# Root-mean-square sums one dq projection later, their diagonals on GpSimd, one 512-column broadcast matmul for each factor

## The chip, the core and the metric

The kernel runs on one core of a Trainium2 chip. The metric is the time of one execution in microseconds (us) on the device; lower is better. TensorE (PE) does matmuls and transposes, VectorE (DVE) and ScalarE (ACT) work on tiles in SBUF and PSUM, GpSimd (POOL) on tiles in SBUF, and SyncE (SP) issues most of the DMAs. Each engine runs its own queue in order, so an instruction that waits holds up all that stands behind it on that engine.

## What is computed

Two transformer layers (`DEPTH = 2`) over 512 tokens of width 1024. Each layer has a mixer of two attention groups (MLA with a low-rank q and kv; DSA with an index score and a top-k choice of keys) and a mixture of 16 experts. What matters here is the beginning of the mixer:

```python
def rms_norm(x, g):
    y = xf * lax.rsqrt(jnp.mean(jnp.square(xf), axis=-1, keepdims=True) + RMS_EPS)
    return (y * g.astype(jnp.float32)).astype(x.dtype)
...
    q = (rms_norm(qa, q_norm_g) @ w_q_up).reshape(B, T, MLA_HEADS, MLA_NOPE + MLA_ROPE)
    c_kv = rms_norm(kva, kv_norm_g)
...
        score = jnp.where(key_idx[None, None, :] <= tq[None, :, None], score, -jnp.inf)
        _, sel = lax.top_k(score, n_keep)
...
    proj = h @ w_in
    qa, kva, kr, dq, dk, dv, iq, ik, iw = jnp.split(proj, SPLIT_POINTS, axis=-1)
```

Here qa has 384 columns, kva 256, dq 512, and `n_keep` is 128.

## The kernel before, in words

All activations are held transposed, features on the partitions and the 512 tokens along the columns. The projection `h @ w_in` is cut into 13 column tiles of 128 features: `proj(ct)` makes one in PSUM with 24 matmuls of 512 columns (`project`, L271: eight slices of the width, each in three products of a high and a low part). The tiles come in the order S, two of iq, DKV, two of kva, three of qa, four of dq. PSUM tiles of the name `mm` rotate through four banks, `pv` through two. SBUF tiles made by `u4` share nine slots, and a tile waits until the last reader of the slot's earlier tile is done.

After qa the squares of kva (`sqk`, the two added up by GpSimd) and of qa (`sqq`, and a part of the tile `dkv`) are summed over the features: matmuls of one column each against ones (L418) put 8 sums for each token of a block on the partitions. In the program this stands in the loop over the four dq tiles at `i == 0`. L421 and L422 (DVE) turn the sums into means plus epsilon, `rsqrt` (L185, GpSimd) takes the power -0.5 of 128 x 8 numbers.

At `i == 2` the factors, which lie along the partitions, are spread over all partitions along the columns: for each of 2 factors and 4 blocks of 128 tokens DVE makes a diagonal matrix (L431, identity times factor), and TensorE multiplies a matrix of ones with it (L432). `bc[0]`, the kv factor, scales `kvg` (L437), which ACT and GpSimd then split into `ckv`. `bc[1]`, the q factor times -96^-0.5, goes into the tile `ct` (L441, L442), by which every q of the MLA heads is multiplied (L528).

Beside all this DVE does the top-k of the DSA group. For query blocks 1, 2 and 3 (tiles of 256, 384 and 512 columns) it runs 16 pairs of MAX8 (L365, the eight largest) and MATCH_REPLACE (L366, strike them out) in strict sequence, and then makes the distance mask `dd` (L372). These pairs have a lowered priority (`LOWER`), so the scheduler fills DVE's queue with them between other work. Each dq tile is read out of PSUM twice: by ACT (L405, the high part) and then by DVE (L406, the low part, which needs ACT's result), and both parts are copied by DMA into the layout of the heads.

The order on every engine is written at build time: a scheduler lists the instructions by priority and by its own estimate of times. Nothing is chosen at run time.

Of the kernel before, what the change touches and what calls it, by code (L numbers as in the profile page):

```python
# [13 lines left out]
AF = mybir.ActivationFunctionType  # L14
OP = mybir.AluOpType
# [3 lines left out]
NT = T // 128  # L19
# [13 lines left out]
SC_MLA = 96.0 ** -0.5  # L33
# [62 lines left out]
def block_kernel(ctx, tc, xT0, x0, win, wqk, wuv, wo, gvec, lnp, rw, rb, wgu, wdn, consts, angles, stripd, rowsd, out):  # L96
    nc = tc.nc
# [19 lines left out]
    def C(name, a=0, b=None):  # L117
        o, w = _C[name]
        return cn[:, o + a:o + (w if b is None else b)]

    ident = C("id")
# [11 lines left out]
    def u4(name, dt=F32):  # L133
        return sl.tile([128, 1024], dt, name=name, tag="u4", bufs=NU4)
# [4 lines left out]
    def u4p(name, dt=F32):  # L139
        t = u4(name, dt)  # L140
        return t[:, :512], t[:, 512:]
# [11 lines left out]
    def ps(tag):  # L153
        return psp.tile([128, 512], F32, name=tag, bufs={"mm": 4, "tr": 2, "pv": 2}[tag])
# [12 lines left out]
    def copy_rows(out, src):  # L167
        nc.sync.dma_start(out.bitcast(F32), src.bitcast(F32))
# [13 lines left out]
    def rsqrt(v, n, tag):  # L182

        y = sm.tile([128, n], F32, name=tag + "y")
        return y, nc.gpsimd.tensor_tensor(y, v, mhalf[:, :n], op=OP.pow).ins  # L185

    def transpose4(src, c0, tag="tr"):
        p = ps(tag)
        for k in range(4):
            last_T[0] = nc.tensor.transpose(p[:, k * 128:(k + 1) * 128], src[:, c0 + k * 128:c0 + (k + 1) * 128],  # L190
                                            ident).ins
        return p
# [38 lines left out]
    def attention(l, xh, xl, wraw, first, rest, x_dram):  # L231
# [10 lines left out]
        def proj(ct):  # L242
            if l and ct == 0:

                raw((3 + AHEAD) // 2)
                for c in range(4):
                    done[c] = ps("mm" if c > 1 else "tr")
                for a in range(2):
                    if a:
                        rest()  # L250
                    for c in (0, 2):
                        order = (0, 1, 2) if a else (0, 2, 1)
                        for j in order:
                            for d in (c, c + 1):
                                project(done[d], first[d], slice(256 * a, 256 * (a + 1)), (j,), order[2])
            if ct not in done:
                done[ct] = ps("mm")
                project(done[ct], weights(ct), slice(0, T))
            return done.pop(ct)
# [16 lines left out]
        acs, acm, adist = at[:, :512], at[:, 512:768].bitcast(BF), at[:, 768:].bitcast(F16)  # L276
# [9 lines left out]
        p = proj(T_S)  # L286
# [9 lines left out]
        for i in range(2):  # L296
            p = proj(T_IQ + i)
# [8 lines left out]
        p = proj(T_DKV)  # L306
# [7 lines left out]
        p = ps("mm")  # L314
# [6 lines left out]
        p = transpose4(dkv, 0)  # L321
        nc.scalar.copy(dvt, p.rearrange("p (a b) -> p a b", a=NT)[:, :, 64:128])
        p = transpose4(S, 0)
# [15 lines left out]
        for i in range(1, NT):  # L339
            n = 128 * (i + 1)  # L340
            acc, work = u4p("aw")
            rel = None
            for h in range(8):
                if (i, h) in KVA_AT:
                    latents(KVA_AT.index((i, h)))
                p = ps("mm")
                nc.tensor.matmul(p[:, :n], iq[h // 4][:, h % 4, (i - 1) * 128:i * 128], ik4[:, :n],
                                 start=True, stop=True)
# [5 lines left out]
                if h == 0:  # L354
                    nc.vector.scalar_tensor_tensor(acc[:, :n], r[:, :n], w, acm[:, 384 - 128 * i:],
                                                   op0=OP.mult, op1=OP.subtract)
                else:
                    nc.vector.scalar_tensor_tensor(acc[:, :n], r[:, :n], w, acc[:, :n],  # L358
                                                   op0=OP.mult, op1=OP.add)
# [10 lines left out]
            for dd in DD[i]:  # L370
# [3 lines left out]
                                               op0=OP.mult, op1=OP.add)  # L374
# [9 lines left out]
        for i in range(3):  # L384
            p = proj(T_QA + i)
# [16 lines left out]
        for i in range(4):  # L402
            p = proj(T_DQ + i)
            qh, ql = u4p("dq", F32R)
            nc.scalar.activation(qh, p, AF.Copy, scale=-0.125)  # L405
            nc.vector.scalar_tensor_tensor(ql, p, -0.125, qh.bitcast(F32), op0=OP.mult, op1=OP.subtract)  # L406
            for s in range(2):
                d = dqs[i // 2][:, i % 2 * 2 + s, :]
                for j, q in enumerate((qh, ql)):
                    b = 64 * (s ^ j)  # L410
                    copy_rows(d[b:b + 64], q[64 * s:64 * (s + 1)])
            if i == 0:

                p = ps("pv")
                for j, qq in enumerate((sqk[:1], sqq)):
                    for t in range(NT):
                        for q in qq:
                            nc.tensor.matmul(p[:, j * 4 + t:j * 4 + t + 1], q[:, t * 128:(t + 1) * 128],  # L418
                                             C("ones", 0, 1), start=(q is qq[0]), stop=(q is qq[-1]))
                ms = sm.tile([128, 8], F32, name="ms")  # L420
                nc.vector.tensor_scalar(ms[:, 0:4], p[:, 0:4], 1.0 / 256, 1e-6, op0=OP.mult, op1=OP.add)  # L421
                nc.vector.tensor_scalar(ms[:, 4:8], p[:, 4:8], 1.0 / 384, 1e-6, op0=OP.mult, op1=OP.add)  # L422
                rs, _ = rsqrt(ms, 8, "rms")
            if i == 2:
                bc = []
                dgt = u4("dg")
                for j, f in ((0, 1.0), (1, -SC_MLA)):
                    p = ps("pv")
                    for t in range(NT):
                        dg = dgt[:, j * 512 + t * 128:j * 512 + (t + 1) * 128]  # L430
                        nc.vector.tensor_scalar(dg, ident, rs[:, j * 4 + t:j * 4 + t + 1], f, op0=OP.mult, op1=OP.mult)  # L431
                        nc.tensor.matmul(p[:, t * 128:(t + 1) * 128], C("ones"), dg, start=True, stop=True)  # L432
                    bc.append(p)
        ckt = bigt(F32R)
        ckv = [(ckt[:, 1024 * i:1024 * i + 512], ckt[:, 1024 * i + 512:1024 * (i + 1)]) for i in range(2)]
# [2 lines left out]
            split(*ckv[i], kvg[i], nc.gpsimd)  # L438
        cte, cto = u4p("ct")
        for c, a, b in ((cte, 0, 64), (cto, 64, 0)):  # L440
            nc.scalar.copy(c[a:a + 64], bc[1][a:a + 64])  # L441
            nc.vector.tensor_mul(c[b:b + 64], acs[b:b + 64], bc[1][b:b + 64])  # L442

        zz = u4("zz")
        with tc.issue_after(anchor):
# [4 lines left out]
        for t in range(NT):  # L450
            p = ps("mm")
# [150 lines left out]
        g, b = ln  # L602
# [5 lines left out]
        p = ps("pv")  # L608
# [127 lines left out]
        for s in range(16):  # L736
            if s >= LAG:
                t, k = 2 * ((s - LAG) // 8) + 1, (s - LAG) % 8
# [11 lines left out]
            t, k = 2 * (s // 8), s % 8  # L750
# [661 lines left out]
    for a, b in [(0, 512), (512, 1024), (1024, 2048), (2048, 3072), (3072, 4096)]:  # L1412
        d = a // 2048, (slice(None), slice(a % 2048, a % 2048 + b - a))
        nc.sync.dma_start(xf[d[0]][d[1]], xT0[:, a:b])
        if a >= w_at:
            c = w_at // 2048, (slice(None), slice(w_at % 2048, w_at % 2048 + 1024))
# [7 lines left out]
    for l in range(L):  # L1424
        r, pre = attention(l, xh, xl, wraw, ws, rest, src)
        y = experts(l, r, pre)
        wraw = pre["win"]
        new = combine(l, r, *y, pre["x1"], wraw)
        if l + 1 < L:
            xh, xl, rest, ws = new  # L1430
        src = x1d
# [59 lines left out]
```

## Time and profile before

| what | us |
| --- | --- |
| median of 3 runs | 1238.58 |
| lowest, highest | 1237.5, 1240.96 |
| profiled execution, its own time | 1238.69 |
| its span in the trace | 1236.9 |

Over the span PE is busy 1168.2 us (94%), DVE 1033.9 (84%), ACT 803.8 (65%), POOL 292.6 (24%). Layer 0 begins at 0 and layer 1 at about 620 us; in each, the stretch that the change touches is some 35 us long (77 to 110 us, 693 to 726 us). A busy PE is not PE at its peak: the ends of matmuls are modelled and they overlap, so the matmuls' start times tell more. The clock that the throttle granted to TensorE is given as a share of full speed.

### The profile page before, as it was taken

The numbers are of one execution on the slowest core, as the hardware profiler recorded it, in microseconds if no ns is written. First come the engines' busy times: TensorE is split into PE (matmuls) and PEld (weight loads), VectorE is DVE, ScalarE is ACT, GpSimd is POOL, SyncE is SP. The second block draws the span as 40 slices with busy tenths as digits, with TensorE's granted clock in tenths as the row PEclk, the third lists the DMA queues.
The fourth block names the chain that finished last, engine by engine and source line by source line (L and its number), as shares of the span: only waits on it lengthen the run. The fifth ranks groups of instructions, "written<-read, shape, count | busy, mean of one in ns | idle before, by whom it ended". The sixth has DMA issues, their size and how long they took to land.

```text
span 1236.9 us, 16946 instructions
## 1 busy us (share of the span) xinstructions
PE 1168.2 (94%) x5777; PEld 918.9 (74%) x5777; DVE 1033.9 (84%) x1875; ACT 803.8 (65%) x1264; POOL 292.6 (24%) x233
## 2 busy tenths in 40 slices
PE   8999999998999999999898998999989999999995
PEld 6677565787788888887686775557877888888873
DVE  4699958398999999988857999673889999999887
ACT  4523668444888888887534245684448888888873
POOL 2334123210211111200543342321201111121005
PEclk9989989999999999999988899999999999999998
DMA  7615204366999999997336161044669999999841
GB/s 269 187 60 172 85 1 137 136 238 236 371 384 392 384 378 377 376 327 272 95 124 167 41 203 43 3 144 164 236 247 368 389 382 390 392 373 362 307 170 68
DMA packets 56972, 292.21 MB, mean 236 GB/s; under 512 B 10063, under 2 KB 13903, under 8 KB 28464
## 3 DMA queue, kind: packets, MB, share of 16 engines
q1 hardware_dynamic: 47376, 270.48, 59.4%
q0 software_dynamic: 8064, 15.36, 3.4%
q10 hardware_dynamic: 1440, 5.24, 1.0%
q8 instruction: 47, 0.77, 0.2%
q14 instruction: 45, 0.37, 0.1%
HBM read 267.96 MB, written 31.98 MB: 242 GB/s over the span
## 4 chain that ended last, share of the span: by engine, by line
PE 56%; DVE 10%; issue 4%; POOL 2%; DMA 2%; ACT 2%; POOLq 0%; DVEq 0%; ACTq 0%
PE pv L1081 14%; PE mm L1059 13%; PE mm L1060 13%; PE tr L190 4%; PE mm L631 3%; PE mm L271 2%; PE pv L509 2%; PE tr L500 2%; DVE aw L366 1%; DMA xg<-xdr,ii 1%; POOL x L1214 1%; DVE m L365 1%; PE mm L543 1%; DVE aw L358 1%; PE pv L655 1%
## 5 line engine op out<-in xcount | busy, mean ns | idle before, releaser
L163 ACT CAST hl<-big 128x1024 fp32r<-128x1024 f32 x438 | 457.6, 1054 | 132.5 <-PE mm L1060 62.7
L164 DVE TENSOR_TENSOR hl<-big,hl 128x1024 fp32r<-128x1024 f32 x403 | 485.8, 1229 | 57.0 <-ACT hl L163 49.4
L1059 PE MATMUL mm<-hl,xh 128*128 128x512 f32 x504 | 207.1, 411 | 0.0
L1060 PE MATMUL mm<-hl,xh 128*128 128x512 f32 x504 | 197.3, 391 | 0.0
L1081 PE MATMUL pv<-hl,hT 128*128 128x512 f32 x720 | 173.0, 395 | 4.1 <-DVE big L1091 4.1
L1081 PEld LDWEIGHTS pv<-hl,hT 128*128 128x128 f32 x720 | 137.2, 191 | 33.9 <-DVE big L1091 4.8
L271 PE MATMUL mm<-big,hl 128*128 128x512 f32 (+1 forms) x624 | 145.2, 392 | 3.1 <-ACT hl L163 1.9
L271 PEld LDWEIGHTS mm<-big,hl 128*128 128x128 f32 x624 | 116.1, 199 | 28.3 <-ACT hl L163 3.9
L164 POOL TENSOR_TENSOR hl<-big,hl 128x1024 fp32r<-128x1024 f32 x35 | 85.4, 2443 | 162.7 <-ACT hl L163 154.4
L1023 POOL DMA_INDIRECT xg<-xdr,ii x30 | 52.4, 1746 | 282.7 <-DVE ii L1037 253.9
L1060 PEld LDWEIGHTS mm<-hl,xh 128*128 128x128 f32 x504 | 95.2, 189 | 15.8
L1059 PEld LDWEIGHTS mm<-hl,xh 128*128 128x128 f32 x504 | 95.0, 188 | 15.5
L1060 PE MATMUL mm<-hl,xl 128*128 128x512 f32 x252 | 98.7, 392 | 0.0
L1059 PE MATMUL mm<-hl,xl 128*128 128x512 f32 x252 | 98.5, 391 | 0.0
L631 PE MATMUL mm<-hl,big 128*128 128x512 f32 x384 | 94.5, 397 | 0.0
L490 ACT ACTIVATE P<-P,mn 128x128 f32<-128x128 f32 (+3 forms) x128 | 71.7, 566 | 13.2 <-DVE mn L488 10.8
L631 PEld LDWEIGHTS mm<-hl,big 128*128 128x128 f32 x384 | 70.3, 188 | 13.2
L502 ACT COPY big<-tr 128x512 f32<-128x512 f32 (+3 forms) x128 | 50.1, 431 | 32.2 <-PE tr L500 31.2
L500 PEld LDWEIGHTS tr<-cn,P 128*128 128x128 f32 x320 | 36.4, 141 | 38.8 <-ACT big L502 21.2
L500 PE MATMUL tr<-cn,P 128*128 128x128 f32 x320 | 59.7, 292 | 4.8 <-DVE P L496 3.2
L570 POOL TENSOR_TENSOR mh<-dd,cn 128x256 f32<-128x256 f32 (+2 forms) x64 | 43.5, 701 | 77.1 <-DVE q L528 21.1
L1101 POOL DMA_INDIRECT ydr<-y,ii x26 | 26.5, 1018 | 146.7 <-ACT y L1097 123.1
(278 smaller groups left out, 1884.7 us busy)
## 6 DMA issues: line engine op xcount, KB each, us to landing
big<-wgu SPq DMA_DIRECT2D x128, 1024.0 KB, 7.7
big<-wdn SPq DMA_DIRECT2D x64, 1024.0 KB, 7.3
big<-win SPq DMA_DIRECT2D x10, 1024.0 KB, 5.8
ydr<-zz SPq DMA_DIRECT2D x2, 4096.0 KB, 13.4
big<-wo SPq DMA_DIRECT2D x8, 1024.0 KB, 9.9
big<-ydr SPq DMA_DIRECT2D x8, 1024.0 KB, 4.9
big<-wqk SPq DMA_DIRECT2D x4, 1024.0 KB, 5.0
big<-dq SPq DMA_DIRECT2D x32, 128.0 KB, 2.3
```

The costliest lines, as they stand in the source:

```text
L163: i = nc.scalar.copy(hi, src).ins
L164: (eng or nc.vector).tensor_sub(lo, src, hi.bitcast(F32))
L190: last_T[0] = nc.tensor.transpose(p[:, k * 128:(k + 1) * 128], src[:, c0 + k * 128:c0 + (k + 1) * 128], ident).ins
L271: nc.tensor.matmul(p[:, ts], w[j == 1][:, k * 128:(k + 1) * 128], x, start=(j + k == 0), stop=(j == end and k == 7))
L490: nc.scalar.activation(e, e, AF.Exp, bias=mn[:, i:i + 1], scale=-1.0, accum_out=su[:, i:i + 1])
L500: nc.tensor.transpose(p[:, (i - kb) * 128:(i - kb + 1) * 128], P[:, PO[i] + kb * 128:PO[i] + (kb + 1) * 128], ident)
L502: copies.append(nc.scalar.copy(pt[kb], p[:, :512 - 128 * kb]).ins)
L631: R["pe"] = nc.tensor.matmul(pp[t][i], x, w[:, i * 512:(i + 1) * 512], start=first, stop=last).ins
L1023: return nc.gpsimd.indirect_dma_start(out=st[e]["xg"], out_offset=None, in_=xdr[l], in_offset=bass.IndirectOffsetOnAxis(ap=st[e]["ii"][:, ...
L1059: nc.tensor.matmul(pg, x, w[:, :512], start=(k == 0 and x is a and w is wh), stop=last)
L1060: nc.tensor.matmul(pu, x, w[:, 512:], start=(k == 0 and x is a and w is wh), stop=last)
L1081: nc.tensor.matmul(py[i], x, w[:, i * 512:(i + 1) * 512], start=(k == 0 and x is a and w is wh), stop=last)
```

## The change

The sums (L418), the means and the power move from the first turn of the dq loop to the second. The diagonals move there too, from DVE to GpSimd: two products of 128 x 512, each with the identity repeated four times as one operand and the factors repeated along the columns as the other. At `i == 2` one matmul of 512 columns for each factor takes the place of four of 128. The constant -96^-0.5 leaves the diagonals and goes into the two instructions that make `ct` (on ACT a scale, on DVE a fused scalar).

```diff
-            if i == 0:
+            if i == 1:
                 p = ps("pv")
 ...
-                nc.vector.tensor_scalar(ms[:, 0:4], p[:, 0:4], 1.0 / 256, 1e-6, op0=OP.mult, op1=OP.add)
-                nc.vector.tensor_scalar(ms[:, 4:8], p[:, 4:8], 1.0 / 384, 1e-6, op0=OP.mult, op1=OP.add)
+                for j, n in enumerate((256, 384)):
+                    nc.vector.tensor_scalar(ms[:, 4 * j:4 * j + 4], p[:, 4 * j:4 * j + 4], 1.0 / n, 1e-6,
+                                            op0=OP.mult, op1=OP.add)
                 rs, _ = rsqrt(ms, 8, "rms")
+                dgt = u4("dg")
+                for j in range(2):
+                    nc.gpsimd.tensor_tensor(dgt[:, j * 512:(j + 1) * 512].rearrange("p (t a) -> p t a", t=NT),
+                                            ident[:, None, :].to_broadcast([128, NT, 128]),
+                                            rs[:, 4 * j:4 * j + 4][:, :, None].to_broadcast([128, NT, 128]), op=OP.mult)
             if i == 2:
                 bc = []
-                dgt = u4("dg")
-                for j, f in ((0, 1.0), (1, -SC_MLA)):
+                for j in range(2):
                     p = ps("pv")
-                    for t in range(NT):
-                        dg = dgt[:, j * 512 + t * 128:j * 512 + (t + 1) * 128]
-                        nc.vector.tensor_scalar(dg, ident, rs[:, j * 4 + t:j * 4 + t + 1], f, op0=OP.mult, op1=OP.mult)
-                        nc.tensor.matmul(p[:, t * 128:(t + 1) * 128], C("ones"), dg, start=True, stop=True)
+                    nc.tensor.matmul(p, C("ones"), dgt[:, j * 512:(j + 1) * 512], start=True, stop=True)
                     bc.append(p)
 ...
-            nc.scalar.copy(c[a:a + 64], bc[1][a:a + 64])
-            nc.vector.tensor_mul(c[b:b + 64], acs[b:b + 64], bc[1][b:b + 64])
+            nc.scalar.activation(c[a:a + 64], bc[1][a:a + 64], AF.Copy, scale=-SC_MLA)
+            nc.vector.scalar_tensor_tensor(c[b:b + 64], bc[1][b:b + 64], -SC_MLA, acs[b:b + 64], op0=OP.mult, op1=OP.mult)
```

The new lines are L422 (means), L427 (diagonals), L434 (broadcast), L439 (`kvg`), L443 and L444 (`ct`); behind these, lines of the changed kernel stand two higher than before (L528 is L530).

How the order moves is seen at three places; both layers read alike there.

First, TensorE around the sums. The rows marked with - are those of before. L271 are the projections (24 a tile: 96 are three qa tiles and the first dq), L418 the sums, of which four (of `sqk`) stand further up in both.

```order
 L347 MATMUL mm<-ik,big 128x512 x3
-L271 MATMUL mm<-big,hl 128x512 x96
+L271 MATMUL mm<-big,hl 128x512 x120
 L418 MATMUL pv<-cn,sqq 128x1 x2
 L418 MATMUL pv<-cn,dkv 128x1
```

The second dq projection now stands ahead of the sums. Behind them, still on TensorE:

```order
 L418 MATMUL pv<-cn,sqq 128x1 x2
 L418 MATMUL pv<-cn,dkv 128x1
-L271 MATMUL mm<-big,hl 128x512 x52
-L432 MATMUL pv<-dg,cn 128x128 x2
-L271 MATMUL mm<-big,hl 128x512 x2
-L432 MATMUL pv<-dg,cn 128x128 x6
-L271 MATMUL mm<-big,hl 128x512 x18
+L271 MATMUL mm<-big,hl 128x512 x24
+L434 MATMUL pv<-dg,cn 128x512 x2
+L271 MATMUL mm<-big,hl 128x512 x24
```

The broadcasts stood inside the fourth dq projection, and now stand between the third and the fourth.

Second, DVE at the means, in query block 2's top-k (the number in a name such as m_493 counts the pairs up). Before:

```order
L365 MAX m_493<-aw 128x8
L421 TENSOR_SCALAR ms<-pv 128x4
L422 TENSOR_SCALAR ms<-pv 128x4
L366 MATCH_REPLACE aw<-m_493,aw 128x384
L365 MAX m_496<-aw 128x8
L406 SCALAR_TENSOR_TENSOR dq<-mm,dq 128x512
```

With the change:

```order
L365 MAX m_493<-aw 128x8
L366 MATCH_REPLACE aw<-m_493,aw 128x384
L365 MAX m_496<-aw 128x8
L366 MATCH_REPLACE aw<-m_496,aw 128x384
L365 MAX m_499<-aw 128x8
L406 SCALAR_TENSOR_TENSOR dq<-mm,dq 128x512
L366 MATCH_REPLACE aw<-m_499,aw 128x384
L365 MAX m_502<-aw 128x8
L366 MATCH_REPLACE aw<-m_502,aw 128x384
L365 MAX m_505<-aw 128x8
L422 TENSOR_SCALAR ms<-pv 128x4 x2
```

The means have moved behind four more pairs and behind the low part of the first dq tile. On GpSimd the split of the weights `wv` (L164), which stood behind the power, now stands ahead of it, and the first L405 on ACT waits for that split, whose slot its tile takes, where it waited for the last sum before.

Third, DVE at the diagonals. Before:

```order
L366 MATCH_REPLACE aw<-m_517,aw 128x384
L431 TENSOR_SCALAR dg<-cn,rmsy 128x128 x2
L406 SCALAR_TENSOR_TENSOR dq<-mm,dq 128x512
L431 TENSOR_SCALAR dg<-cn,rmsy 128x128 x6
L437 TENSOR_TENSOR kvg<-kvg,pv 128x512 x2
L365 MAX m_520<-aw 128x8
```

With the change:

```order
L366 MATCH_REPLACE aw<-m_517,aw 128x384
L365 MAX m_520<-aw 128x8
L406 SCALAR_TENSOR_TENSOR dq<-mm,dq 128x512
L439 TENSOR_TENSOR kvg<-kvg,pv 128x512 x2
L366 MATCH_REPLACE aw<-m_520,aw 128x384
```

The eight diagonals have left DVE's queue. Further down the fourth L406 stands two instructions later than before (a mask L372 and a replace of 512 columns have come ahead of it), one more pair of 512 columns stands ahead of the first q (L528, now L530), and in the middle heads PE, DVE, ACT and POOL have another order: the mask of query block 3 comes ahead of a q product and a weight split that stood ahead of it before. From the last heads on, the order is the same again.

## Rows read from the trace of the kernel before

**Rows 1.** Stretches: us, busy PE PEld DVE ACT POOL, PEclk, DMA share, GB/s.

```profile
77.40:110.50 33.10, 28.59 (x116) 23.84 (x117) 28.31 (x70) 9.17 (x15) 14.58 (x8) 0.79 0.21 48
110.50:160.00 49.50, 45.74 (x193) 31.26 (x193) 45.34 (x128) 28.34 (x74) 17.30 (x20) 0.94 0.38 139
305.00:620.00 315.00, 306.84 (x1517) 251.32 (x1516) 292.85 (x357) 254.84 (x300) 60.18 (x40) 0.99 0.89 337
```

**Rows 2.** Chain that ended last, layer 1: start us, us, what.

```profile
715.13 2.35 DVE dg L431
```

**Rows 3.** Timeline of DVE, layer 0: start, us, instruction [idle before <-releaser].

```profile
84.98 0.16 DVE L421 TENSOR_SCALAR ms<-pv 128x4 f32<-128x4 f32 x1 [0.28 <-PE pv L418]
...
87.48 0.56 DVE L365 MAX8 m<-aw 128x8 f32<-128x384 f32 x1
...
88.73 0.56 DVE L365 MAX8 m<-aw 128x8 f32<-128x384 f32 x1
...
93.52 0.69 DVE L406 SCALAR_TENSOR_TENSOR dq<-mm,dq 128x512 fp32r<-128x512 f32 x1 [2.31 <-ACT dq L405]
...
99.00 0.48 DVE L431 TENSOR_SCALAR dg<-cn,rmsy 128x128 f32<-128x128 f32 x2
...
99.99 3.41 DVE L431 TENSOR_SCALAR dg<-cn,rmsy 128x128 f32<-128x128 f32 x6
...
110.51 0.69 DVE L406 SCALAR_TENSOR_TENSOR dq<-mm,dq 128x512 fp32r<-128x512 f32 x1 [1.35 <-ACT dq L405]
...
113.82 0.68 DVE L365 MAX8 m<-aw 128x8 f32<-128x512 f32 x1
...
115.32 0.69 DVE L365 MAX8 m<-aw 128x8 f32<-128x512 f32 x1
...
118.23 0.68 DVE L528 TENSOR_TENSOR q<-mm,ct 128x512 f32<-128x512 f32 x1
```

**Rows 4.** Timeline of DVE, layer 1, the same places.

```profile
708.57 0.69 DVE L406 SCALAR_TENSOR_TENSOR dq<-mm,dq 128x512 fp32r<-128x512 f32 x1 [1.63 <-ACT dq L405]
...
714.05 0.48 DVE L431 TENSOR_SCALAR dg<-cn,rmsy 128x128 f32<-128x128 f32 x2
...
715.04 3.40 DVE L431 TENSOR_SCALAR dg<-cn,rmsy 128x128 f32<-128x128 f32 x6
...
725.56 0.69 DVE L406 SCALAR_TENSOR_TENSOR dq<-mm,dq 128x512 fp32r<-128x512 f32 x1 [1.08 <-ACT dq L405]
...
733.28 0.68 DVE L528 TENSOR_TENSOR q<-mm,ct 128x512 f32<-128x512 f32 x1
```

**Rows 5.** Timeline of PE, layer 0.

```profile
54.90 21.95 PE L271 MATMUL mm<-big,hl 128*128 128x512 f32 x96
77.49 0.38 PE L418 MATMUL pv<-cn,sqq 128*128 128x1 f32 x2 [0.64 <-ACT sqq L389]
...
80.52 0.59 PE L418 MATMUL pv<-cn,dkv 128*128 128x1 f32 x2 [1.99 <-ACT dkv L389]
...
84.80 14.33 PE L271 MATMUL mm<-big,hl 128*128 128x512 f32 x52
...
195.24 1.02 PE L543 MATMUL mm<-ke,q 128*128 128x512 f32 x2
```

**Rows 6.** Costliest lines, shapes apart, POOL: busy us, mean ns of one, idle before.

```profile
L570 POOL TENSOR_TENSOR mh<-dd,cn 128x384 f32<-128x384 f32 x32 | 27.8, 887 | 77.1 <-DVE q L528 21.1 <-DVE rc L492 18.8 <-DVE mn L488 18.7
...
L164 POOL TENSOR_TENSOR big<-kvg,big 128x512 fp32r<-128x512 f32 x4 | 5.1, 1287 | 5.0 <-ACT big L163 5.0
...
L185 POOL TENSOR_TENSOR rmsy<-ms,mhalf 128x8 f32<-128x8 f32 x2 | 3.3, 1654 | 6.1 <-DVE ms L422 6.1
```

**Rows 7.** Timeline of POOL, layer 0.

```profile
79.68 2.36 POOL L164 TENSOR_TENSOR hl<-big,hl 128x1024 fp32r<-128x1024 f32 x1 [9.39 <-ACT hl L163]
...
99.99 2.35 POOL L164 TENSOR_TENSOR hl<-big,hl 128x1024 fp32r<-128x1024 f32 x1 [3.10 <-ACT hl L163]
```

**Rows 8.** Timeline of DVE, layer 0, behind the last mask of the top-k.

```profile
156.59 0.69 DVE L488 CUSTOM_DVE_ANT_0 P<-mm,mh 128x512 f32<-128x512 f32 x1 [1.22 <-POOL mh L570]
```

## Prediction

> **What bounds the kernel now.** I read the busy times by stretch first. In the stretch from the first means to the fourth dq tile of layer 0 no engine is full: TensorE is busy 28.6 of 33.1 us at a granted clock of 0.79, so that it ran partly at the lower of its two levels, and VectorE 28.3 us [rows 1]. From there to 160 us VectorE is busy 45.3 of 49.5 us, 92%, with top-k pairs between the work of the heads [rows 1]. In the experts (305 to 620 us) TensorE is busy 306.8 of 315 us at 0.99 [rows 1]. So VectorE's queue sets the pace of attention until the top-k is done, and what is gained there reaches the end of the run: behind it stands TensorE's own work, which starts that much earlier, with DMA at 0.89 of its time and not full. The chain of waits says the same from the other end: it runs through VectorE's diagonals for 2.35 us in layer 1 [rows 2].
>
> The timeline of VectorE then shows where its queue stood still. In layer 0 it waits 0.28 us for the sums, 2.31 for the second dq tile and 1.35 for the fourth [rows 3]; in layer 1, 1.63 and 1.08 [rows 4]. On TensorE the reader sees why: the sums come while ACT is still squaring, so TensorE waits 0.64 and then 1.99 us, and the last 20 sum matmuls take from 80.52 to 84.80, 0.21 us each, at a lowered clock [rows 5]. The 52 projections behind them take 14.33 us, 0.276 each, where 96 undisturbed ones took 21.95, 0.229 each [rows 5]. The second dq tile is late by all of this.
>
> **The change, part by part.** All times are of layer 0 unless said otherwise.
>
> *Diagonals off VectorE.* The eight L431 take 0.48 + 3.41 = 3.89 us [rows 3], in layer 1 0.48 + 3.40 = 3.88 [rows 4]. Two of them alone take 0.24 each, the six 0.57 each, because one waits: the six and a GpSimd split of 2.35 us both start at 99.99 [rows 3, 7]. The whole 3.89 leaves the queue.
>
> *The second dq tile ahead of the sums.* TensorE ends the first dq tile and may start the second at about 77.49, when ACT's squaring frees the bank that the first sum waited for too [rows 5]. 24 matmuls at 0.229 are 5.5 us: 83.0. ACT's squares were ready by 80.52 [rows 5], so the sums no longer wait. There are 24 of them; at 0.19 each (0.38 for two, rows 5) to 0.21 they take 4.6 to 5.1 us: I take 88.1. So the second tile is in PSUM at 83.0 where VectorE comes to it at about 91, and the waits of 2.31 (1.63 in layer 1) and 0.28 go. The first tile's eviction now stands behind the split of `wv`: GpSimd's split ahead of it ends at 82.0 [rows 7], this one takes as long, 84.4, and the eviction is done at about 85, before VectorE comes to it at 87. That costs nothing.
>
> *The means are later.* VectorE reached them at 84.98 - 0.28 = 84.70. Now four pairs of 1.25 us (87.48 to 88.73) and one L406 of 0.69 stand ahead [rows 3]: 90.4. TensorE has the sums at 88.1, so nothing waits, but the power comes at 90.4 + 1.65 [rows 6] = 92.1 and not at 86.9. Behind it GpSimd's queue holds two weight splits for the heads; with the diagonals below and 2.36 each they end near 99.5, ahead of a first q that comes at 111.9 at the earliest (below).
>
> *Diagonals on GpSimd.* No row shows this product with both operands repeated. Nearest is the product of the same size with two full operands, 1.29 us; below lies the 128 x 384 mask product with one repeated operand, 0.89 [rows 6]; above, twice the elements, 2.36 [rows 7]. I take 1.29: ready at 93.4 and 94.7; with the bounds the second is ready at 93.9 or 96.8.
>
> The Trainium skill speaks against this part: its page "GPSIMD Engine Reference", section 4.1 Engine selection, keeps two-input products on a tile on VectorE, since GpSimd takes about twice as long. By it, an estimate from the unhindered eighths, the pair would take 2 x 8 x 0.24 = 3.8 us and not 2.6, and the fourth dq tile would come 1.2 us later. The sum below has room for most of that.
>
> *Broadcasts.* A 128 x 512 product in full precision takes 1.02 us (two instructions, rows 5); half the clock would make 2.0. TensorE ends the third dq tile at 88.1 + 5.5 = 93.6, or, with all of the slow excess of the earlier projections (14.33 - 52 x 0.229 = 2.4), at 96.0. The second broadcast ends 1.0 behind the later of its diagonal and the first broadcast: 95.7 to 98.1.
>
> *The fourth dq tile.* 5.5 us at full clock, 7.9 with the excess of 2.4, which I count once: it is in PSUM between 101.2 and 103.6, evicted by ACT 0.6 us later (an L405 like VectorE's 0.69 in size): 101.8 to 104.2. VectorE reached its wait at 110.51 - 1.35 = 109.16; without 3.89 + 2.31 + 0.28 that is 102.7, and a mask and a replace (together 1.3 us by the pair's 1.25) have come ahead: 104.0. So the wait of 1.35 (1.08 in layer 1) goes too, by a margin of 0 to 2 us. With diagonals of 2.36 and the slow excess the tile is evicted at 106.4, and a wait of 2.4 us takes the old one's place: that is the low bound.
>
> *`ct`, `kvg`.* A copy with a scale on ACT, and a fused product on VectorE in place of a plain one: L406, fused, takes 0.69 on twice the partitions and L528, plain, 0.68 [rows 3]. I take nothing; VectorE would show a tenth of a us at most. The zero fill and weight loads behind the dq copies on SP's queue move up with VectorE's L406.
>
> *Sum on VectorE.* Layer 0: 3.89 + 2.31 + 0.28 + 1.35 = 7.8 us; layer 1: 3.88 + 1.63 + 1.08 = 6.6. Together 14.4. The first q gains less, since one more pair of 512 columns, 1.50 us (113.82 to 115.32, rows 3), stands ahead of it: from 118.23 to 111.9 and from 733.28 to 728.2 [rows 3, 4], together 11.4. The heads' chain starts with the first q, and the top-k that paces it ends 14.4 earlier; between the two I take the middle, 12.9. From the profiled execution's 1238.69 that is 1225.8. Its time is 0.1 from the median of the runs, and lies 1.8 over its span, which I leave as it is.
>
> **The low and the high end.** Low gain: 11.4 less a wait of 2.4 in each layer, 6.6. High gain: 14.4, and the stalls at the end of the top-k, where VectorE waits 1.22 for GpSimd's masks [rows 8], go in both layers and for as long again on TensorE: 14.4 + 4.9 = 19.3.
>
> **The rivals.**
>
> *The heads' new order gives part back.* The middle heads are re-ordered, and the block 3 mask comes at another place. For it: there the engines already wait for each other, 1.22 us in one place [rows 8]. Against: the mask is ready earlier. Two more such waits in each layer are 4.9 us: gain 8.0, time 1231.
>
> *TensorE takes VectorE's place, so that little is left.* If the wait for GpSimd's diagonals drops the clock for the whole fourth tile (24 x 0.457 = 11.0) and the diagonals cost 2.36, the tile is evicted at 96.8 + 1.0 + 11.0 + 0.6 = 109.4; VectorE waits 5.4 us, and 2.4 and 1.2 us are left in the layers: 3.6, time 1235, within what a run can tell from no change. For it: a wait of 1.99 was followed by slow matmuls before [rows 5]. Against: the excess there was 2.4, not 5.5, and the wait is shorter now.
>
> *Slower: repeated operands are dear on GpSimd.* If both products are read element by element at some slow rate, the fourth tile is late. The gain of layer 0 is gone when its eviction ends at 104.0 + 7.8 = 111.8, so the second diagonal at 104.7, which is 6.3 us for each product; in layer 1, 5.7. At 10 us each the layers lose 7.4 and 8.6: 1255. Against: the mask product repeats one operand at 0.89 us for 384 columns [rows 6].
>
> **How the numbers follow.** The three measured runs lie 0.28% apart, so I call 0.3%, 3.7 us, the least that can be told. Gain of 10 to 17: 0.60. More than 17, up to the high end: 0.06. The heads give part back (4 to 10): 0.19. Little is left (within 3.7): 0.10. Slower: 0.05. Faster is 0.85, same 0.10, slower 0.05. The time is that of the first case, 1226; 8 in 10 lie between gains of 4.7 and 18.7, that is 1220 to 1234, and the first case's own range is 1222 to 1229.
>
> **What would show it.** Right: in the changed profile VectorE has no L431, the second and fourth L406 come without a wait, the sums (L418) start at about 83 with no idle time ahead, L427 takes about 1.3 us, the first L530 starts near 112 and 728, the granted clock in 77 to 105 us lies above 0.79, and the experts start some 6 us earlier in layer 0 and 13 in layer 1. Wrong: a wait of L434 for L427 of more than 3 us, a wait of the fourth L406, or new waits between 140 and 200 us in the heads.

## The result

| | before | changed |
| --- | --- | --- |
| median, us | 1238.04 (4 runs, 1236.83 to 1240.96) | 1225.22 (4 runs, 1224.46 to 1227.12) |
| ratio, 95% interval | | 0.9891 [0.9866, 0.9916] |
| span of the profiled run, us | 1236.9 | 1222.7 |

The change gains 12.8 us, and the prediction (1226) holds in time, range and sign. A second series of the changed kernel, below, gave 0.9859. The profile shows how far the way there was the predicted one.

VectorE's queue in layer 0, with the start and the length of each entry in us, then the instruction, and in brackets idle time ahead of it with what ended it:

```profile
88.62 0.67 DVE L406 SCALAR_TENSOR_TENSOR dq<-mm,dq 128x512 fp32r<-128x512 f32 x1
...
91.59 0.21 DVE L422 TENSOR_SCALAR ms<-pv 128x4 f32<-128x4 f32 x2
...
92.84 0.67 DVE L406 SCALAR_TENSOR_TENSOR dq<-mm,dq 128x512 fp32r<-128x512 f32 x1
...
98.30 0.67 DVE L406 SCALAR_TENSOR_TENSOR dq<-mm,dq 128x512 fp32r<-128x512 f32 x1
98.89 1.27 DVE L439 TENSOR_TENSOR kvg<-kvg,pv 128x512 f32<-128x512 f32 x2
...
105.18 0.68 DVE L406 SCALAR_TENSOR_TENSOR dq<-mm,dq 128x512 fp32r<-128x512 f32 x1
...
113.15 0.68 DVE L530 TENSOR_TENSOR q<-mm,ct 128x512 f32<-128x512 f32 x1
```

L431 is gone, and no entry has a bracket: neither the second nor the fourth dq tile (L406) is waited for, where [rows 3] had 0.28, 2.31 and 1.35. The first L406 comes 2.4 us later than the 86.25 of before, of which 1.5 lies ahead of the change (below). In layer 1 too no entry has a bracket, and the first q (L530) stands at 719.09, against 733.28 [rows 4].

TensorE in the same place:

```profile
85.21 0.50 PE L418 MATMUL pv<-cn,sqq 128*128 128x1 f32 x4
...
87.81 5.75 PE L271 MATMUL mm<-big,hl 128*128 128x512 f32 x24
94.71 2.12 PE L434 MATMUL pv<-dg,cn 128*128 128x512 f32 x4 [1.16 <-POOL dg L427]
96.27 6.05 PE L271 MATMUL mm<-big,hl 128*128 128x512 f32 x24
```

The sums start at 85.21 without a wait. From there to 87.81 are 24 of them, 2.6 us or 0.11 each, where [rows 5] had 0.21. Two broadcasts take 1.56 from start to start. The one new wait, 1.16 us for GpSimd's diagonal, is 0.18 in layer 1. The granted clock goes with the sums: it was 0.50 from 80.52 to 84.80 before and is 1.00 from 85.2 to 87.8 now. Over the whole stretch it is 1.00, against 0.79 in [rows 1] (the columns are those of [rows 1]):

```profile
77.40:110.50 33.10, 31.95 (x149) 25.69 (x148) 32.04 (x77) 14.72 (x22) 19.70 (x12) 1.00 0.35 91
110.50:160.00 49.50, 43.58 (x202) 27.58 (x202) 43.65 (x128) 27.68 (x79) 15.02 (x19) 0.97 0.29 110
```

Layer 1 differs here. Its sums run at 1.00 too, but the third dq tile behind them takes 7.36 us and not 5.75, at a granted clock of 0.74 from 695 to 700 us; VectorE waits for nothing all the same.

```profile
693.10 7.36 PE L271 MATMUL mm<-big,hl 128*128 128x512 f32 x24
```

GpSimd, with the power (L185) and the two diagonals (L427), 1.02 us each:

```profile
91.88 1.66 POOL L185 TENSOR_TENSOR rmsy<-ms,mhalf 128x8 f32<-128x8 f32 x1 [5.95 <-DVE ms L422]
93.61 2.04 POOL L427 TENSOR_TENSOR dg<-cn,rmsy 128x512 f32<-128x512 f32 x2
95.61 4.74 POOL L164 TENSOR_TENSOR hl<-big,hl 128x1024 fp32r<-128x1024 f32 x2
```

**The ledger.** From the first top-k pair of block 2 (L365), the first q, the last matmul group of the router (L655, now L657) and the first of the experts (L1059, now L1061), read in both traces, the 14.2 us between the spans divide so (us):

| from, to | layer 0, before | after | gain | layer 1, before | after | gain |
| --- | --- | --- | --- | --- | --- | --- |
| start to first pair | 77.39 | 78.88 | -1.5 | | | |
| first pair to first q | 40.84 | 34.27 | 6.6 | 39.79 | 34.27 | 5.5 |
| first q to router | 164.97 | 162.40 | 2.6 | 163.89 | 161.30 | 2.6 |
| router to experts | 12.57 | 14.51 | -1.9 | 14.12 | 16.24 | -2.1 |
| experts to next layer's first pair, or end | 397.72 | 394.76 | 3.0 | 325.61 | 326.07 | -0.5 |

Attention, from the first pair to the router, gains 9.1 and 8.1 us, more than the 7.8 and 6.6 of the sum. The experts start 5.7 us earlier in layer 0 and 14.7 in layer 1, where the prediction had 6 and 13. The 3.0 us of the experts of layer 0 can't be put down to the change: that stretch took from 392.2 to 398.5 us in the ten traces of this document, and the two of the changed kernel lie 2.5 apart. And 1.9 and 2.1 us are given back ahead of the experts. There the same matmuls run at the lower of TensorE's two levels. Before:

```profile
282.23 1.14 PE L720 MATMUL mm<-oh,x 128*128 128x128 f32 x8
283.20 0.96 PE L655 MATMUL pv<-wgb,xt 128*128 128x16 f32 x8
284.01 2.92 PE L720 MATMUL mm<-oh,x 128*128 128x128 f32 x24
```

After:

```profile
274.00 1.76 PE L722 MATMUL mm<-oh,x 128*128 128x128 f32 x8
275.55 1.73 PE L657 MATMUL pv<-wgb,xt 128*128 128x16 f32 x8
277.12 4.85 PE L722 MATMUL mm<-oh,x 128*128 128x128 f32 x24
```

Forty matmuls take 4.5 us (282.23 to 286.77) before and 7.8 (274.00 to 281.80) after. The granted clock of the first 4.8 us of it is 1.00 before and 0.53 after. In both traces TensorE had been busy but for 0.24 us just ahead; the change touches nothing there.

### The profile page after: what moved, and what is told of

The parts are those of the page before. It is cut to its first block, busy times and chain, and to the rows that moved or that the text cites. A ratio compares the mean times of both kernels' runs of the same rounds, so it can differ in the third digit from the quotient of the medians.

```text
span 1222.7 us, 16875 instructions
## 1 busy us (share of the span) xinstructions
PE 1160.0 (95%) x5753; PEld 910.2 (74%) x5753; DVE 1027.7 (84%) x1859; ACT 802.6 (66%) x1264; POOL 298.5 (24%) x237
## 5 line engine op out<-in xcount | busy, mean ns | idle before, releaser
L164 DVE TENSOR_TENSOR hl<-big,hl 128x1024 fp32r<-128x1024 f32 x403 | 484.6, 1226 | 58.2 <-ACT hl L163 51.0
L1061 PE MATMUL mm<-hl,xh 128*128 128x512 f32 x504 | 207.4, 412 | 0.0
L271 PE MATMUL mm<-big,hl 128*128 128x512 f32 (+1 forms) x624 | 142.7, 387 | 2.3 <-ACT hl L163 1.2
L271 PEld LDWEIGHTS mm<-big,hl 128*128 128x128 f32 x624 | 114.4, 195 | 28.0 <-ACT hl L163 2.9
L164 POOL TENSOR_TENSOR hl<-big,hl 128x1024 fp32r<-128x1024 f32 x35 | 84.7, 2424 | 134.4 <-ACT hl L163 120.1
L1061 PEld LDWEIGHTS mm<-hl,xh 128*128 128x128 f32 x504 | 95.2, 189 | 15.7
L1061 PE MATMUL mm<-hl,xl 128*128 128x512 f32 x252 | 98.7, 392 | 0.0
```

The costliest lines, as they stand in the source:

```text
L164: (eng or nc.vector).tensor_sub(lo, src, hi.bitcast(F32))
L271: nc.tensor.matmul(p[:, ts], w[j == 1][:, k * 128:(k + 1) * 128], x, start=(j + k == 0), stop=(j == end and k == 7))
L1061: nc.tensor.matmul(pg, x, w[:, :512], start=(k == 0 and x is a and w is wh), stop=last)
```

## The experiments

Each was timed beside the kernel before on the same chip; gains are against its median there (1239.31 and 1239.92 us). The first edit is shown against the kernel before, the others against the changed kernel.

**Only the sums moved.**

```diff
-            if i == 0:
+            if i == 1:
                 p = ps("pv")
```

> Of the change, only the place of the sums: they and the means stand behind the second dq projection; the eight diagonals stay on VectorE (L431), and the eight broadcast matmuls of 128 columns stay. Theory of the prediction (each wait is a term of its own): the waits 2.31 + 0.28 and 1.63 us go, the 3.9 us of diagonals and the waits for the fourth dq tile stay, so 4.2 us are gained: some 1234 us against 1238, and the sums start with no idle time ahead. Rival (what mattered was TensorE's clock, lowered behind its waits of 0.64 and 1.99 us, and not VectorE's queue): with the waits gone the clock in 77 to 105 us is 1.0 and most of the whole gain is here already, 9 us or more: below 1229 us.

1233.56 us (11 runs), ratio 0.9955 [0.9938, 0.9972]: the theory's time, with a gain of 5.7 us where it had 4.2. The time rules the rival's 9 us out. It does not say what an unbroken clock would be worth, since the clock still falls, to 0.72 at 86 to 92 and at 96 to 102 us; the two traces of the changed kernel say it for the stretch behind the diagonals (below). And the terms are not as separate as I took them. VectorE:

```profile
96.84 0.92 DVE L431 TENSOR_SCALAR dg<-cn,rmsy 128x128 f32<-128x128 f32 x1
97.68 0.68 DVE L406 SCALAR_TENSOR_TENSOR dq<-mm,dq 128x512 fp32r<-128x512 f32 x1
98.28 1.45 DVE L431 TENSOR_SCALAR dg<-cn,rmsy 128x128 f32<-128x128 f32 x7
101.21 1.28 DVE L437 TENSOR_TENSOR kvg<-kvg,pv 128x512 f32<-128x512 f32 x2 [1.48 <-PE pv L432]
...
106.98 0.67 DVE L406 SCALAR_TENSOR_TENSOR dq<-mm,dq 128x512 fp32r<-128x512 f32 x1
...
108.41 2.57 DVE L372 SCALAR_TENSOR_TENSOR dd<-aw,at 128x384 f32<-128x384 f32 x1
```

The first diagonal takes 0.92 us while GpSimd splits a weight tile (95.33 to 97.68), the other seven 0.21 each behind it: 2.4 us, not 3.89. So some 1.5 us of that term was the overlap with GpSimd's split, and goes with the sums' place alone. The wait for the fourth dq tile, which the theory kept, is gone as well. Against these stand a new wait, 1.48 us of `kvg` for the broadcast, and 2.0 us of the mask L372, which takes 2.57 us beside another split of GpSimd (108.17 to 110.57) where before it took 0.56; in layer 1 both are there too. So the time agrees with the theory, and its terms do not.

**All but GpSimd:** sums moved, one broadcast of 512 columns for each factor, the diagonals on VectorE.

```diff
+            if i == 2:
+                bc = []
                 dgt = u4("dg")
                 for j in range(2):
-                    nc.gpsimd.tensor_tensor(dgt[:, j * 512:(j + 1) * 512].rearrange("p (t a) -> p t a", t=NT),
-                                            ident[:, None, :].to_broadcast([128, NT, 128]),
-                                            rs[:, 4 * j:4 * j + 4][:, :, None].to_broadcast([128, NT, 128]), op=OP.mult)
-            if i == 2:
-                bc = []
-                for j in range(2):
                     p = ps("pv")
+                    for t in range(NT):
+                        nc.vector.tensor_scalar(dgt[:, j * 512 + t * 128:j * 512 + (t + 1) * 128], ident,
+                                                rs[:, j * 4 + t:j * 4 + t + 1], 1.0, op0=OP.mult, op1=OP.mult)
                     nc.tensor.matmul(p, C("ones"), dgt[:, j * 512:(j + 1) * 512], start=True, stop=True)
```

> All of the change but GpSimd: sums behind the second dq projection, one broadcast matmul of 512 columns for each factor, and the diagonals still eight products on VectorE. Theory of the prediction: the broadcast's form is worth nothing by itself, so the time is that of the kernel with the sums alone moved, some 1234 us, and 8 us of the 13 are still missing (7.8 of diagonals). Rival (fewer matmul instructions between the projections are worth time): 1 to 2 us less for each layer, 1230 to 1232 us.

1229.73 us (6 runs), 0.9933 [0.9908, 0.9958]: nearer to the rival. The wait of `kvg` is 0.46 us in layer 0 and gone in layer 1, so the form is worth something, 1.0 and 1.5 us by that wait. It is not all of the difference: in layer 0 the mask L372 takes 0.56 us again, not 2.57 (in layer 1 it takes 2.49), since it begins just ahead of GpSimd's split, and a wait of 0.66 us for the fourth dq tile is new. The intervals of this and the run before overlap, so the 3.8 us between the medians are not all settled.

**The other half:** the changed kernel with the sums back behind the first dq tile.

```diff
-            if i == 1:
+            if i == 0:
                 p = ps("pv")
```

> The other half of the change: the sums stay behind the first dq projection, the diagonals are two products of GpSimd and the broadcasts one matmul of 512 columns for each factor. Theory (the terms of the prediction add up): 3.9 us of diagonals leave VectorE in each layer, the waits of 2.31 and 1.63 us for the second dq tile stay, and of the waits for the fourth some 1 us stays, so that 8 us are gained: 1230 to 1231 us, and together with the 5.7 us of the sums alone this makes the whole change. Rival (TensorE, still slowed behind the sums, takes VectorE's place): the fourth dq tile waits 3 us or more, half of the gain is lost, 1234 us.

1227.84 us (6 runs), 0.9896 [0.9874, 0.9919]: 12.1 us gained, more than either theory gave. The wait for the second dq tile stays as foreseen; of that for the fourth nothing stays:

```profile
86.90 0.67 DVE L406 SCALAR_TENSOR_TENSOR dq<-mm,dq 128x512 fp32r<-128x512 f32 x1
...
94.70 0.69 DVE L406 SCALAR_TENSOR_TENSOR dq<-mm,dq 128x512 fp32r<-128x512 f32 x1 [2.84 <-ACT dq L405]
...
108.05 0.68 DVE L406 SCALAR_TENSOR_TENSOR dq<-mm,dq 128x512 fp32r<-128x512 f32 x1
```

2.84 us for the second dq tile (2.46 in layer 1), none for the fourth. By the queue that is 3.89 + 1.35 less 0.5 of longer waits, 4.7, in layer 0 and 3.88 + 1.08 less 0.8, 4.1, in layer 1: 8.8 and not the 8 expected. The trace gains 11.4 from the first pair to the router, so that 2.6 are no term of the queue; they go with the earlier end of the top-k (the table below). Whether the halves add up can't be told: by the medians 12.1 and 5.7 are 17.8, against 12.8 and 16.7 for the whole, and by the traces 11.4 and 3.3 are 14.7, against 17.2 and 16.8. GpSimd's half is the larger.

**GpSimd's products done twice, and six times** (the same values written again).

```diff
-                for j in range(2):
+                for j in [j for j in range(2) for _ in range(2)]:   # 6 in the second kernel
                     nc.gpsimd.tensor_tensor(dgt[:, j * 512:(j + 1) * 512]...
```

> The changed kernel with each product of GpSimd done twice (the same values written again): 4.1 us more before the second broadcast than the 2.0 us that the pair took. Theory of the prediction (there is room: the fourth dq tile is evicted well before VectorE comes to it at 105.2 us): second diagonal at 97.7 instead of 95.65, broadcasts done at 98.5, fourth tile evicted at 105.1; no wait, the time stays at 1225 us. Rival (TensorE's longer wait, some 3 us, drops its clock): the fourth tile takes 11 us instead of 5.5, VectorE waits 5 us for it in each layer, 1235 us.

1224.3 us (6 runs), 0.9883 [0.9862, 0.9903]: no cost that can be told in the time. (The four products take 4.04 us, 2.0 more than the pair; the 4.1 of the expectation is the whole.) The build alternated the two factors' products, so the first diagonal came last but one. TensorE waits 3.81 us for it, and its clock falls, but only for part of the tile:

```profile
96.41 3.78 PE L434 MATMUL pv<-dg,cn 128*128 128x512 f32 x4 [3.81 <-POOL dg L427]
99.21 7.47 PE L271 MATMUL mm<-big,hl 128*128 128x512 f32 x24
```

The tile behind it takes 7.30 us (99.21 to the next group at 106.51) where the changed kernel's first trace has 5.88 (96.27 to 102.15), and VectorE waits 1.49 us for it in layer 0, where the theory had no wait, and not at all in layer 1. From the first pair to the router this trace is 2.3 to 2.8 us behind the two traces of the changed kernel in layer 0, and level with them in layer 1.

> The changed kernel with each product of GpSimd done six times, 6.1 us for a factor, 12.2 for both. Theory of the prediction: its threshold was 6.3 and 5.7 us for a factor, so that nothing of the gain is left: the second diagonal at 105.9, the fourth tile evicted at some 113, VectorE waits 7 to 8 us in each layer, 1238 to 1241 us. Rival 1 (a longer wait drops TensorE's clock, on top of the delay): some 1248 us. Rival 2 (VectorE takes top-k pairs ahead and so hides the delay): 1230 us or less.

1241.91 us (12 runs), 1.0033 [1.0016, 1.0051]: close to the theory's 1238 to 1241, and neither rival's. Nothing of the gain is left with the second diagonal at 105.0, where the prediction had 104.7. But the wait is elsewhere:

```profile
97.69 0.67 DVE L406 SCALAR_TENSOR_TENSOR dq<-mm,dq 128x512 fp32r<-128x512 f32 x1
106.17 1.28 DVE L439 TENSOR_TENSOR kvg<-kvg,pv 128x512 f32<-128x512 f32 x2 [7.82 <-PE pv L434]
...
114.06 0.69 DVE L406 SCALAR_TENSOR_TENSOR dq<-mm,dq 128x512 fp32r<-128x512 f32 x1 [0.49 <-ACT dq L405]
```

It is `kvg` that waits, 7.82 us (7.80 in layer 1), and the fourth dq tile is waited for only 0.49 (1.02). Since the products alternate, the first factor was as late as the second here.

**Only the second factor's product six times.**

```diff
-                for j in range(2):
+                for j in (0,) + (1,) * 6:
```

> The changed kernel with the second factor's product done six times (the same values), the first factor's once: the first diagonal is as early as before, the second comes at some 103 us in layer 0, 7.5 us later. VectorE's products with the first factor (L439) need not wait, only the fourth dq tile is late. Theory (the fourth tile is what sets the limit, as in the prediction): broadcast to 103.9, tile to 109.4, eviction at 110.0, VectorE comes at 105.2 and waits 4.8 us in each layer: 1235 us, and 1238 us if TensorE's clock falls in the wait. Rival (in the run with six products for each factor it was only the late first factor, for which L439 waited 7.8 us, that cost the gain): no wait worth the name, 1225 to 1227 us.

1236.02 us (12 runs, 1230.45 to 1242.47), 0.9976 [0.9952, 1.0]: the theory's. The profiled execution is the fastest of the twelve, and no run comes down to the rival's 1225 to 1227. In its profile:

```profile
97.62 1.28 DVE L439 TENSOR_TENSOR kvg<-kvg,pv 128x512 f32<-128x512 f32 x2
...
112.22 0.69 DVE L406 SCALAR_TENSOR_TENSOR dq<-mm,dq 128x512 fp32r<-128x512 f32 x1 [6.37 <-ACT dq L405]
```

`kvg` does not wait, and the fourth dq tile is late by 6.37 us (6.25 in layer 1). The theory had 4.8; the clock fell behind TensorE's wait for the diagonal, to 0.72 from 103.3 to 111.5 us, and the tile took 8.2 us. So there are two deadlines: the first factor's for `kvg`, the second's for the fourth tile, and the prediction named only the second.

**The changed kernel once more.**

> The changed kernel once more, unchanged, beside the others. Its first profile shows TensorE's clock low ahead of the experts (L722) in both layers, 3 us of lost time each, which the profile of before does not. Theory (where the clock falls in this stretch differs from execution to execution): in this profile the falls stand elsewhere, or in one layer only, and the time lies between 1221 and 1229 us. Rival (the fall ahead of the experts belongs to the changed kernel's order): both falls are there again.

1223.25 us (6 runs), 0.9859 [0.9833, 0.9884]. The theory fell: both falls are there again.

```profile
273.36 2.05 PE L722 MATMUL mm<-oh,x 128*128 128x128 f32 x8
275.20 1.73 PE L657 MATMUL pv<-wgb,xt 128*128 128x16 f32 x8
276.77 5.47 PE L722 MATMUL mm<-oh,x 128*128 128x128 f32 x24
```

They are not the changed kernel's own either. The fall at this place (these matmuls at more than half as long again) is in both layers in this run and with the sums back, in layer 0 alone with VectorE's diagonals and with both kernels of repeated products for two factors, in layer 1 alone with only the sums moved, and in neither layer before, with the second factor's product repeated, and in the run below. Within one kernel it came back; what decides it stays open.

This trace also settles what the clock behind the diagonals is worth. TensorE waits 1.78 us for them, its granted clock is 0.72 from 94 to 100 us, and the fourth dq tile takes 7.28 us, where the first trace has 6.05. VectorE's queue does not feel it:

```profile
93.93 2.98 PE L434 MATMUL pv<-dg,cn 128*128 128x512 f32 x4 [1.78 <-POOL dg L427]
95.92 7.28 PE L271 MATMUL mm<-big,hl 128*128 128x512 f32 x24
```

```profile
104.40 0.68 DVE L406 SCALAR_TENSOR_TENSOR dq<-mm,dq 128x512 fp32r<-128x512 f32 x1
...
112.38 0.68 DVE L530 TENSOR_TENSOR q<-mm,ct 128x512 f32<-128x512 f32 x1
```

The first q comes 34.29 us behind the first pair (78.09) and the end of the top-k 62.29; in the first trace it is 34.27 and 62.26. So a fall of this size behind the diagonals costs VectorE nothing, and the gain does not rest on an unbroken clock there. What the low clock at the sums of before adds to the wait for the second dq tile, no run shows by itself.

**More taken off VectorE.**

```diff
+        nc.scalar.copy(dgt[:, 0:512], bc[0])
 ...
-            nc.vector.tensor_mul(kvg[i], kvg[i], bc[0])
+            nc.gpsimd.tensor_mul(kvg[i], kvg[i], dgt[:, 0:512])
 ...
-            nc.scalar.activation(c[a:a + 64], bc[1][a:a + 64], AF.Copy, scale=-SC_MLA)
-            nc.vector.scalar_tensor_tensor(c[b:b + 64], bc[1][b:b + 64], -SC_MLA, acs[b:b + 64], op0=OP.mult, op1=OP.mult)
+            nc.scalar.activation(c, bc[1], AF.Copy, scale=-SC_MLA)
+            nc.gpsimd.tensor_mul(c[b:b + 64], c[b:b + 64], acs[b:b + 64])
```

> The changed kernel with more taken off VectorE: ACT copies the first factor's broadcast out of PSUM, GpSimd multiplies the two kvg tiles by it; ACT evicts the whole of both ct tiles with the scale, GpSimd multiplies their halves by the angles. VectorE loses 2 x 0.64 + 2 x 0.69 = 2.7 us in each layer. Theory (VectorE's queue still sets the pace up to the end of the top-k): 5 us are gained over the changed kernel, 1220 us. Rival (with VectorE's waits gone, TensorE and the heads are now as late as it): nothing is gained, 1224 to 1226 us, and new waits stand in the heads between 113 and 200 us.

1214.59 us (5 runs, 1212.21 to 1214.88), 0.9786 [0.9767, 0.9804]: 25 us less than before and 8.7 less than the changed kernel in the same series (10.6 less than in the first), better than theory and rival. More than the 5 us of VectorE's queue needs an account: against the changed kernel's second trace, from the first pair to the router it gains 3.5 and 1.8 us, 5.3 together, as the theory has it. Another 4.6 lie between router and experts, where no fall stands here, and 2.8 are lost in the other stretches; no run shows that these come of the edit. GpSimd pays 2.55 us for `kvg` and 2.66 for `ct`, and VectorE waits for neither:

```profile
100.02 2.55 POOL L440 TENSOR_TENSOR kvg<-kvg,dg 128x512 f32<-128x512 f32 x2
...
106.79 2.66 POOL L445 TENSOR_TENSOR ct<-ct,at 64x512 f32<-64x512 f32 x2
```

## Why the prediction was right, step by step

**VectorE sets the pace: right, and its two ends price it.** The prediction took the middle between the gain of the first q and that of the top-k's end. The traces can be held to this: from the first pair to the first q, and to the comparison that ends block 3's top-k (L368). The rows for layer 0, before:

```profile
77.39 0.55 DVE L365 MAX8 m<-aw 128x8 f32<-128x384 f32 x1
...
152.26 0.68 DVE L368 TENSOR_TENSOR aw<-aw 128x512 f32<-128x512 f32 x1
```

and after:

```profile
78.88 0.54 DVE L365 MAX8 m<-aw 128x8 f32<-128x384 f32 x1
...
141.14 0.69 DVE L368 TENSOR_TENSOR aw<-aw 128x512 f32<-128x512 f32 x1
```

74.87 us before, 62.26 after: 12.6 (12.0 in layer 1), far above the 7.8 (6.6) of the sum. The rest, 4.8 and 5.4, is no saving: between first q and top-k's end VectorE does less head work than before. In layer 0 it has four L528 products where it had six (1.4 us), one head's four L488 fewer with their accumulators (2.3), and one weight split fewer (1.4): some 5 us that no longer stand ahead of the top-k's end. That is why, in the changed kernel, the end of the top-k overstates the gain, and the first q understates it. Gains in us, both layers together; the fourth column of numbers is read in the same trace as the first three, the last is that of the times:

| kernel | first q | end of top-k | middle | first pair to router | median gained |
| --- | --- | --- | --- | --- | --- |
| only the sums | 4.8 | 4.0 | 4.4 | 3.3 | 5.7 |
| all but GpSimd | 9.3 | 7.8 | 8.6 | 8.1 | 9.6 |
| the other half | 5.0 | 17.5 | 11.3 | 11.4 | 12.1 |
| changed, two series | 12.1 | 24.6 | 18.4 | 17.2, 16.8 | 12.8, 16.7 |
| products twice | 8.6 | 21.1 | 14.8 | 14.4 | 15.0 |
| products six times | -7.4 | 5.1 | -1.2 | -1.6 | -2.6 |
| second factor six times | -4.5 | 8.0 | 1.8 | 3.7 | 3.9 |
| more off VectorE | 9.9 | 34.8 | 22.4 | 22.1 | 25.3 |

In every trace the middle lies within 2 us of what attention gained up to the router. This is a rule found in these kernels, not derived. The median of the times is further off, by up to 5.6 us: the falls ahead of the experts and the uneven time of the experts stand between the two.

For the changed kernel my middle, 12.9, came from a top-k's end put too near; with the measured end it is 18.4, attention gained 17.2, and the 4.0 us lost ahead of the experts bring it down again. So the time was right partly by luck, because two errors met: **the step that failed is "the top-k that paces it ends 14.4 earlier"** (24.6), and the give-back has another place and cause than the rival's masks in the heads.

**Diagonals off VectorE, 3.89: right in the queue, wrong as a price of its own.** It contains some 1.5 us of overlap with GpSimd, which moving the sums takes away too.

**The second dq tile ahead of the sums: right,** no idle time on VectorE or TensorE. The sums were over-priced, 2.6 us for 4.6 to 5.1, since they ran at a granted clock of 1.00; VectorE waited for none of them.

**Means and power: right.** L422 at 91.59 is 1.2 behind the 90.4 forecast, with 1.5 of late start in it; VectorE's means still wait for nothing. GpSimd's weight splits behind the diagonals end at 100.35 (95.61 + 4.74; 99.5 forecast), far ahead of the first q.

**Diagonals on GpSimd, 1.29: a little high** (1.02), between the bounds. The rule of the Trainium skill's page "GPSIMD Engine Reference" (4.1 Engine selection), that VectorE does a two-input product in about half the time, is not borne out for the diagonals: four eighths on VectorE take 0.83 us (4 of the seven in 1.45), in a form with one tile and one scalar for each partition, and GpSimd's product 1.02. For `kvg` and `ct` it is: GpSimd takes 1.28 us for each `kvg` and 1.33 for each `ct` in the last run, and VectorE takes 0.64 and 0.69 in the changed kernel. Even diagonals at twice 1.02 us cost no more than 2.3 to 2.8 us in one layer.

**Broadcasts 1.02 each: high,** 0.78. **The fourth dq tile by a margin of 0 to 2 us: right.** In the second trace of the changed kernel it is in PSUM at 103.2 (95.92 + 7.28), its eviction takes 0.60 (to 103.8), and VectorE comes at 104.40; in the first trace the eviction ends at 103.0 and VectorE comes at 105.18.

**The rivals.** TensorE did not take VectorE's place: its wait for the new work was 1.16 us. Heads that give part back did not show, since the way from the first q to the router got 2.6 us shorter in each layer. GpSimd's products would have to cost six times what they do to lose the gain. The forecast "first L530 near 728" forgot layer 0's own gain: the first q of layer 1 comes 14.2 us earlier, 8.7 of them because the layer starts earlier, and the 5.5 left stand against the 5.1 forecast.

## What to carry to other kernels

Where one engine does long filler work (a top-k) between the steps of a chain, price a change by two marks, the chain's next step and the end of the filler, and expect the gain of that stretch between them; the fixed order trades one for the other. Costs read while two engines overlap belong partly to the overlap: 1.5 of the 3.89 us of diagonals went with another edit. Ask of work moved to another engine for each result when its first user comes: here 2 us more on GpSimd cost nothing that could be told in the time, and a further move of the same kind gained 5.3 us more in attention. And read a gain in the stretch that the edit touches, in the same trace: here other stretches added or took up to 5.5 us.

## What the runs showed of the hardware

VectorE instructions slow down beside GpSimd, some more than others. L431 took 0.21 us alone and 0.92 when it began beside a GpSimd split. The mask L372, with two operands in SBUF, took 0.54 us in the changed kernel and 1.05 (at 111.86) beside a GpSimd split (109.61 to 112.49) in the run with six products for each factor; MAX8 of 384 columns took 0.54 to 0.56 throughout. How dear it is depends on how much of the split is left: the mask ended 0.4 us behind the split's end in that run, and so it did where it began early in the split and took 2.57 us (108.41 to 110.98, split to 110.57, only the sums moved). Where the mask began first (108.85, split at 108.91, all but GpSimd) it kept its 0.56, and the split took 2.76 us for 2.40. The page "SBUF — State Buffer" of the Trainium skill (Who interferes with whom) says that VectorE's second port pair is shared with GpSimd, and that instructions with one SBUF input outside its two-port modes don't contend; these rows agree with it.

TensorE's clock fell behind waits of 1.8 us (94 to 100 us in the second trace of the changed kernel) and not behind one of 1.16 us in the first. It also fell with no such wait ahead: behind the sums in layer 1 of the changed kernel (0.74 from 695 to 700 us), where TensorE had not waited at all, and ahead of the experts, where it had waited 0.24 us, in some kernels and not in others, at 1.4 to 3.1 us a layer. That is as much as a good edit is worth, and what decides it stays open.
